# Four of eight modulation chunks: their products written for GpSimd instead of TensorE

## The chip, the cores and the metric

One core of one Trainium2 chip runs the kernel. Its engines run in parallel and each works through its own instructions in order: TensorE (PE in the profile, with its weight loads as PEld), VectorE (DVE), ScalarE (ACT), GpSimd (POOL), and SyncE (SP), whose queue issues the DMAs of this kernel. An instruction starts when everything it waits for, by semaphores, has happened; what stands behind it on its engine waits with it. The metric is the device time of one launch in microseconds (us), as the median of several runs. Times inside a run are from its profile and count from the start of the profiled span.

## The reference, cut to what matters

Two transformer blocks run one after the other on 512 tokens of width 1024. In the first one the vector `c` yields six modulation rows of 1024 numbers each. Two of them (`sh1`, `sc1`) shape the input of the attention; the other four are used after it:

```
m_lat = jax.nn.silu(c) @ w_mod[l] + b_mod[l]
sh1, sc1, g1, sh2, sc2, g2 = jnp.split(m_lat[:, None, :], 6, axis=-1)
...
y = merge_branches(proj, att, ...)      # gates, attention and convolution branches, output projection
x_mid = x + g1 * y
h2 = modulate(rmsnorm(x_mid, norm_ffn[l]), sh2, sc2)
f = hierarchical_moe(h2, ...)           # 32 experts, each a SwiGLU
x = x_mid + g2 * f
```

`w_mod` is 1024 x 6144 in float32. A row of the modulation is made in two chunks of 512 columns; a chunk needs 1024 x 512 weights (2 MB, in two loads of 1 MB), eight products of 128 x 512 with a number for each partition, and a sum over the 128 partitions, which at the same time spreads the row to all partitions.

## The kernel before

The kernel is written in program order; every engine gets its instructions in the order of the code, and a planner of the buffers gives each tile a place in one of 23 buffers of 8 KB a partition (pool `w`) or 6 of 4 KB (pool `h`). A DMA waits on SP until the earlier user of its buffer is done, and the DMAs behind it wait with it.

After the convolution's work, the last of 16 attention steps (`attention`, `s_work`) are interleaved with the gate projections `ga0` to `gb7` (`gate_proj`: eight k-steps of three matmuls each, and a tanh on ACT), and then the branch projections `ao0` to `ao7` follow (the loop over `i` with `pys`). Each of these takes a unit of the weight stream: SP loads it raw (`ga6r`), ACT rounds it to a high part and DVE makes the low part (`ga6p`, L200 and L270), and PE multiplies with both. `mr` is a tile with a chunk's sum in its first quarter and the bias row in its fourth; `bcs0` and `bcs1` hold the finished rows; `sil` holds silu of `c`.

The modulation's chunks go through these steps as a side job: `mod_run(n)` advances the generator `modr` by n steps, at most two in an attention step from number 13 on, four after each half of the gates 6 and 7, and one after each half of a branch. Eight chunks run one after the other, `g1`, `sc2`, `sh2`, `g2`, two each. A chunk of the first four has its eight products on DVE (L773, L775), is split into two parts there (`mt`, L202 and L207), and is summed over the partitions by two matmuls with ones (`mb`, L786 and L787). A chunk of the last four (`MOD_PE`) has its products on PE: eight matmuls in float32 (`mp`, L760, two instructions of each in the trace), a copy on ACT and a float32 matmul that sums (`mb`, L768). In both cases DVE then adds the bias row into `bcs` (L788). GpSimd computes nothing.

What comes behind is the output projection, the routing, the experts, whose 192 MB of weights are loaded as buffers come free, and the second block.

Of the kernel before, what the change touches and what calls it, by code (L numbers as in the profile page):

```python
# [9 lines left out]
F32R = mybir.dt.float32r  # L10
# [3 lines left out]
ALU = mybir.AluOpType  # L14
# [21 lines left out]

IN_H = [f"{nm}{n}" for nm in ("k_", "q_", "u_") for n in range(4)] + [f"m1{f}" for f in range(2, 32)]
N_HALF, N_LAST = 2, 4
MOD_PE = range(4, 8)
N_EARLY, N_PRE = 7, 15  # L40
N_KQ, N_V, N_C, N_A, N_M, N_MR, N_G, N_AO = 4, 1, 9, 7, 13, 2, 4, 1
WROW = 8
# [14 lines left out]
C_ID, C_TRI, C_ONE, C_SEL2, C_IOTA, C_RCNT, C_EOF, C_SELB, C_IOM8, C_IOM4, NC_ = 0, 128, 256, 384, 386, 514, 578, 706, 834, 842, 846  # L57
# [105 lines left out]
def body(ctx, tc, a, out, dbg=None):  # L163
# [8 lines left out]
    def slot(shape, name, dt=F32):  # L172

        return wpool.tile([P] + list(shape), dt, name=name, tag="w")

    def hslot(shape, name, dt=F32):

        return hpool.tile([P] + list(shape), dt, name=name, tag="h")

    def const(shape, name, dt=F32):  # L180
        return cpool.tile([P] + list(shape), dt, name=name)

    def bank(name, shape=(512,), parts=P):
        return pp.tile([parts] + list(shape), F32, name=name, tag="ps")
# [96 lines left out]
    cst = const([NC_], "cst")  # L281
# [26 lines left out]
    sil = const([KD, 32], "sil")  # L308
# [8 lines left out]
    ones_r = const([P], "ones_r", F32R)  # L317
# [425 lines left out]
    def mod_rows(n):
        nm, c = mod_todo[n]
        ch = mod_of[nm] + c
        if n == 0:
            mod_load(0, 0)
            mod_load(0, 1)
        cs = slice(512 * c, 512 * c + 512)
        t = slot([4, 512], f"mr{ch}")  # L750
        acc = t[:, 0]
        ld(t[:, 3], a["b_mod"][:, ch * 512:ch * 512 + 512].to_broadcast([P, 512]))
        if nm == "sc2" and c == 1:
            nf = slot([D], "nf")
            ld(nf, a["norm_ffn"].to_broadcast([P, D]))
        yield
        if n in MOD_PE:
            pm = bank(f"mp{ch}")
            for k in range(KD):
                mm(pm[32 * (k % 4):32 * (k % 4) + 32], sil[:, k, :], mod_w[n, k // 4][:, k % 4, :],  # L760
                   start=(k < 4), stop=(k >= 4), tile_position=(0, 32 * (k % 4)), skip_group_check=True)
                if k % 4 == 3:
                    del mod_w[n, k // 4]
                    mod_load(n + 1, k // 4)
# [4 lines left out]
        else:
            for k in range(KD):  # L770
                src = mod_w[n, k // 4][:, k % 4, :]
                if k == 0:
                    V.tensor_scalar(acc, src, sil[:, k, 0:1], None, op0=ALU.mult)  # L773
                else:
                    V.scalar_tensor_tensor(acc, src, sil[:, k, 0:1], acc, op0=ALU.mult, op1=ALU.add)  # L775
                if k % 4 == 3:
                    del mod_w[n, k // 4]
                    mod_load(n + 1, k // 4)
                if k % 2:
                    yield  # L780
            t2 = hslot([2, 512], f"mt{ch}", F32R)
            split(acc, t2[:, 0], t2[:, 1], V)
            yield
            yield
            ps = bank(f"mb{ch}")
            mm(ps, ones_r, t2[:, 0], start=True, stop=False)  # L786
            mm(ps, ones_r, t2[:, 1], start=False, stop=True)  # L787
        V.tensor_tensor(bc[nm][:, cs], ps, t[:, 3], op=ALU.add)  # L788
        if c == 1:
            if nm in ("g1", "g2"):  # L790
                V.tensor_scalar(bc[nm], bc[nm], 0.5, None, op0=ALU.mult)
            if nm == "sc2":
                V.scalar_tensor_tensor(bc[nm], bc[nm], 1.0, nf, op0=ALU.add, op1=ALU.mult)
        yield

    modr = chain(mod_rows(n) for n in range(len(mod_todo)))

    def mod_run(n):
        for _ in range(n):
            if next(modr, 0) == 0:  # L800
                return
# [47 lines left out]
    for i in range(8):  # L849
# [439 lines left out]
    for i, ps_ in enumerate(PASSES):  # L1289
# [28 lines left out]
        c = 0  # L1318
# [593 lines left out]
```

## Time and profile before

| what | us |
|---|---|
| median of 3 runs | 1513.46 (1513.39 to 1514.01) |
| the profiled execution | 1514.14 |
| its span, from the first to the last instruction | 1512.4 |
| PE busy | 1405.2 (93%) |
| DVE busy | 787.1 (52%) |
| ACT busy | 455.6 (30%) |
| POOL busy | 0.2, in 4 instructions |

The busy time of an engine is the time in which at least one of its instructions ran. Matmuls are pipelined: one of 128x512 stands with 0.39 us in the trace while the next one starts 0.23 us after it. The granted clock is the share of TensorE's full clock that it ran at. A wait is put down to what ended it last.

### The profile page before, as it was taken

To read this page: it belongs to the slowest core of one execution; us is meant where nothing else is said; L and a number is where in the kernel's file an instruction comes from. 1 tells how busy PE (TensorE), PEld (TensorE's weight loads), DVE (VectorE), ACT (ScalarE), POOL (GpSimd) and SP (SyncE) were. 2 spreads that over 40 slices of the span, in tenths; PEclk is the share of its full clock that TensorE was granted. 3 is DMA by queue.
4 is the path that set the end of the run, shared out by engine and by line. 5 is a ranking of instruction groups with operands and counts; after the bars stand their busy time and mean duration, and the time that the engine had idled before them with its cause. 6 is when DMAs were issued, how large, how long until landed. Compare 5 with 4: busy or idle time off the path is not lost. (4 is left out here: it accounts for less than half of the span.)

```text
span 1512.4 us, 18758 instructions
## 1 busy us (share of the span) xinstructions
PE 1405.2 (93%) x7398; PEld 973.0 (64%) x7398; DVE 787.1 (52%) x1559; ACT 455.6 (30%) x787; POOL 0.2 (0%) x4
## 2 busy tenths in 40 slices
PE   5999999999987989979999798899999999999997
PEld 4788877786773525334534254677678888878886
DVE  6387887586478423322333133746757443354326
ACT  4252566623231101101111012447723222343300
POOL 0000000000000000000000000000000000000000
PEclk9999999999997999989999899899999999999998
DMA  9232020688655899999999995131510222443301
GB/s 392 109 98 111 32 95 5 222 322 292 245 210 226 337 417 420 419 419 419 419 419 420 419 419 212 54 149 45 179 55 29 98 98 98 153 140 112 111 1 56
DMA packets 53243, 320.51 MB, mean 212 GB/s; under 512 B 6168, under 2 KB 6424, under 8 KB 21280
## 3 DMA queue, kind: packets, MB, share of 16 engines
q1 hardware_dynamic: 53152, 319.28, 54.0%
q8 instruction: 59, 0.97, 0.3%
q14 instruction: 32, 0.26, 0.0%
HBM read 317.15 MB, written 2.11 MB: 211 GB/s over the span
## 5 line engine op out<-in xcount | busy, mean ns | idle before, releaser
L1282 PE MATMUL pU<-wu,xT 128*64 128x512 f32 (+1 forms) x544 | 115.8, 638 | 22.1 <-DMA wu<-in_w_exp_up_dram 22.1
L1282 PE MATMUL py<-wd,mt 128*64 128x512 f32 (+1 forms) x544 | 107.6, 637 | 12.8 <-DMA wd<-in_w_exp_down_dram 7.6
L1282 PE MATMUL pG<-wg,xT 128*64 128x512 f32 (+1 forms) x544 | 95.5, 594 | 3.4 <-DMA wg<-in_w_exp_gate_dram 3.4
L1282 PEld LDWEIGHTS pU<-wu,xT 128*64 128x64 f32 (+1 forms) x544 | 32.5, 130 | 102.0 <-issue 57.9
L440 DVE SCALAR_TENSOR_TENSOR cacc<-u,cw,cacc 128x511 f32<-128x511 f32 (+14 forms) x120 | 89.1, 743 | 3.6
L1282 PEld LDWEIGHTS py<-wd,mt 128*64 128x64 f32 (+1 forms) x544 | 30.0, 131 | 81.5 <-issue 55.9
L1282 PEld LDWEIGHTS pG<-wg,xT 128*64 128x64 f32 (+1 forms) x544 | 29.7, 124 | 66.5 <-issue 56.9
L1734 DVE TENSOR_TENSOR hid<-rl 128x512 f32<-128x512 f32 x32 | 22.1, 692 | 96.2 <-ACT rl L1733 96.2
L1188 DVE TENSOR_TENSOR mt<-mt,pU 128x512 f32<-128x512 f32 x13 | 8.9, 688 | 110.9 <-PE pU L1282 110.8
L200 ACT ACTIVATE Cr<-pC 128x512 fp32r<-128x512 f32 x13 | 7.8, 598 | 187.0 <-PE pf L1204 179.4
L1205 DVE TENSOR_TENSOR xr<-xr,pf 128x512 f32<-128x512 f32 x96 | 58.4, 678 | 6.9 <-PE pf L1204 6.9
L1171 PE MATMUL px<-Db,yh 128*128 128x256 f32 x224 | 56.5, 292 | 2.6 <-DVE Db L1157 1.4
L576 ACT ACTIVATE at<-at,mx 128x512 f32<-128x512 f32 (+4 forms) x64 | 39.9, 624 | 62.5 <-DVE mx L665 28.4
L1733 ACT ACTIVATE rl<-m 128x512 f32<-128x512 f32 x32 | 19.1, 598 | 120.7 <-PE m L212 120.7
L1171 PE MATMUL px<-Db,yl 128*128 128x256 f32 x224 | 55.5, 287 | 0.0
L1197 DVE SCALAR_TENSOR_TENSOR mt<-py,gsl,bcs 128x512 f32<-128x512 f32 x26 | 19.5, 751 | 68.8 <-PE py L1282 68.7
L200 ACT ACTIVATE yb<-mt 128x512 fp32r<-128x512 f32 x26 | 16.4, 629 | 114.9 <-DVE mt L1197 114.9
L1187 DVE SCALAR_TENSOR_TENSOR mt<-mt,pG 128x512 f32<-128x512 f32 x13 | 8.9, 687 | 72.4 <-ACT mt L1186 72.4
L1171 PEld LDWEIGHTS px<-Db,yh 128*128 128x128 f32 x224 | 43.7, 195 | 4.3 <-ACT Cr L200 2.4
L1171 PEld LDWEIGHTS px<-Db,yl 128*128 128x128 f32 x224 | 43.8, 195 | 0.0
L1203 PE MATMUL pf<-yb,Cr 128*128 128x512 f32 x96 | 38.6, 402 | 0.0
L1204 PE MATMUL pf<-yb,Cr 128*128 128x512 f32 x96 | 37.6, 392 | 0.0
(1330 smaller groups left out, 3498.8 us busy)
## 6 DMA issues: line engine op xcount, KB each, us to landing
wg<-in_w_exp_gate_dram SPq DMA_DIRECT2D x64, 1024.0 KB, 19.8
wu<-in_w_exp_up_dram SPq DMA_DIRECT2D x64, 1024.0 KB, 19.8
wd<-in_w_exp_down_dram SPq DMA_DIRECT2D x64, 1024.0 KB, 19.8
wmod<-in_w_mod_dram SPq DMA_DIRECT2D x24, 1024.0 KB, 6.4
bias<-in_bias_dram SPq DMA_DIRECT2D x4, 896.0 KB, 5.3
x<-in_x_rows_dram SPq DMA_DIRECT2D x2, 1024.0 KB, 6.8
mr<-in_b_mod_dram SPq DMA_DIRECT2D x8, 256.0 KB, 5.9
xr<-in_x_rows_dram SPq DMA_DIRECT2D x2, 1024.0 KB, 7.2
```

The lines of the kernel that those rows point to most:

```text
L200: S.activation(dst, src, AF.Copy)
L440: V.scalar_tensor_tensor(cacc[:, i, lo_:hi_], u[:, i, lo_ + d:hi_ + d], w1, cacc[:, i, lo_:hi_], op0=ALU.mult, op1=ALU.add)
L576: S.activation(sb[:, 0:nk], sb[:, 0:nk], AF.Exp, bias=mx[:, s, 0:1], scale=score[2], accum_out=mx[:, s, 1:2])
L1171: mm(ps[:, k % 2], h_[t // 2][:, t % 2, k * P:(k + 1) * P], rhs, start=(k % 2 + t + n == 0), stop=(t == NT - 1 and n == 1), skip_group_che ...
L1187: V.scalar_tensor_tensor(t_, t_, 1.0, pG, op0=ALU.add, op1=ALU.mult)
L1197: V.scalar_tensor_tensor(yf, ps, gsl, bc["g2"][:, cs], op0=ALU.mult, op1=ALU.mult)
L1203: mm(ps, C[:, t * P:(t + 1) * P], y[0][:, cs], start=True, stop=False)
L1204: mm(ps, C[:, t * P:(t + 1) * P], y[1][:, cs], start=False, stop=True)
L1205: V.tensor_tensor(xrow[t][:, cs], xrow[t][:, cs], ps, op=ALU.add)
L1282: mm(ps[c:c + w], lhs[:, c:c + w], rhs(p), start=start, stop=stop, skip_group_check=True)
L1733: S.activation(r, ps, AF.Relu)
L1734: V.tensor_tensor(hid[f // 4][:, f % 4, :], r, r, op=ALU.mult)
```

## The change

The four chunks of `sh2` and `g2` are taken out of `modr`, which keeps `g1` and `sc2` (all on DVE), and go to a new generator, `pool_rows`. For each chunk it issues eight `tensor_scalar` and seven `tensor_tensor` on GpSimd (128x512, float32), each waiting for the one before it where it reads its result. DVE splits the finished chunk, PE sums it with two matmuls with ones, and DVE adds the bias, as the chunks of `modr` do. The first statement of `mod_run` advances `pool_rows` by one step in every call, so its chunks begin with the last attention steps; before, their matmuls were issued with the branches. The float32 matmuls `mp` and `mb` with `C_SELB` and the copies on ACT are gone.

```diff
-MOD_PE = range(4, 8)
-    mod_todo = [(nm, c) for nm in names for c in range(2)]
+    mod_todo = [(nm, c) for nm in ("g1", "sc2") for c in range(2)]
...
-        if n in MOD_PE:
-            pm = bank(f"mp{ch}")
-            for k in range(KD):
-                mm(pm[32 * (k % 4):32 * (k % 4) + 32], sil[:, k, :], mod_w[n, k // 4][:, k % 4, :],
...
-            copy(S, acc, pm)
-            yield
-            ps = bank(f"mb{ch}")
-            mm(ps, cst[:, C_SELB:C_SELB + P], acc, start=True, stop=True)
...
+    def pool_rows(todo):
+        old, w = None, {}
+        def load(n):
+            nm, c = todo[n]
+            w[n] = [load_mod(mod_of[nm] + c, half) for half in range(2)]
+        load(0)
+        yield
+        for n in range(len(todo) + 1):
+            if n < len(todo):
+                nm, c = todo[n]
+                ch = mod_of[nm] + c
+                t = slot([4, 512], f"mr{ch}")
+                ld(t[:, 3], a["b_mod"][:, ch * 512:ch * 512 + 512].to_broadcast([P, 512]))
+                for k in range(KD):
+                    src = w[n][k // 4][:, k % 4, :]
+                    G.tensor_scalar(t[:, min(k, 1)], src, sil[:, k, 0:1], None, op0=ALU.mult)
+                    if k:
+                        G.tensor_tensor(t[:, 0], t[:, 0], t[:, 1], op=ALU.add)
+                del w[n]
+                new = nm, c, ch, t
+            yield
+            if n + 1 < len(todo):
+                load(n + 1)
+            if old:
+                nm_, c_, ch_, t_ = old
+                t2 = hslot([2, 512], f"mt{ch_}", F32R)
+                split(t_[:, 0], t2[:, 0], t2[:, 1], V)
+                yield
+                ps = bank(f"mb{ch_}")
+                mm(ps, ones_r, t2[:, 0], start=True, stop=False)
+                mm(ps, ones_r, t2[:, 1], start=False, stop=True)
+                V.tensor_tensor(bc[nm_][:, 512 * c_:512 * c_ + 512], ps, t_[:, 3], op=ALU.add)
+                if nm_ == "g2" and c_:
+                    V.tensor_scalar(bc[nm_], bc[nm_], 0.5, None, op0=ALU.mult)
+            old = new
...
+    modp = pool_rows([(nm, c) for nm in ("sh2", "g2") for c in range(2)])
     def mod_run(n):
+        next(modp, 0)
...
     mod_run(100)
+    for _ in modp:
+        pass
```

In the tiles' names the number after `wmod`, `mr`, `mt` or `mb` is the chunk: 4 and 5 are `g1`, 8 and 9 `sc2`, 6 and 7 `sh2`, 10 and 11 `g2`; `_0` and `_1` are a chunk's two loads. SP's queue, at the first loads of the modulation, before:

```order
L295 DMA wmod4_0_2159<-in_w_mod_dram 128x2048 [waits DVE_49]
L295 DMA wmod4_1_2161<-in_w_mod_dram 128x2048 [waits DMAHW6_49,PE_49]
L752 DMA mr4_2163<-in_b_mod_dram 128x512 [waits DMAHW7_49,PE_49]
L254 DMA ga5r_2191<-in_stream1_dram 128x1024 [waits DMAHW0_49]
L295 DMA wmod5_0_2239<-in_w_mod_dram 128x2048 [waits DMAHW1_49,PE_49,Activation_49]
L254 DMA gb5r_2266<-in_stream1_dram 128x1024 [waits DMAHW2_49]
L295 DMA wmod5_1_2313<-in_w_mod_dram 128x2048 [waits DMAHW5_49,DMAHW3_49,DVE_49]
L254 DMA ga6r_2340<-in_stream1_dram 128x1024 [waits DMAHW4_49]
L254 DMA gb6r_2395<-in_stream1_dram 128x1024
```

The same queue now, from the bias row of the first GpSimd chunk on (the two loads of chunk 6 and those of chunk 4 stand ahead of it):

```order
L797 DMA mr6_2241<-in_b_mod_dram 128x512 [waits DMAHW3_49,PE_49]
L294 DMA wmod5_0_2260<-in_w_mod_dram 128x2048 [waits DMAHW7_49,DMAHW4_49,DVE_49]
L253 DMA gb5r_2287<-in_stream1_dram 128x1024 [waits DMAHW5_49]
L294 DMA wmod7_0_2332<-in_w_mod_dram 128x2048 [waits DMAHW6_49,DVE_49]
L294 DMA wmod7_1_2334<-in_w_mod_dram 128x2048 [waits PE_49,Activation_49]
L797 DMA mr7_2336<-in_b_mod_dram 128x512 [waits DMAHW0_49,Pool_49]
L294 DMA wmod5_1_2355<-in_w_mod_dram 128x2048 [waits DMAHW1_49,DVE_49]
L253 DMA ga6r_2382<-in_stream1_dram 128x1024 [waits DMAHW2_49]
L294 DMA wmod10_0_2411<-in_w_mod_dram 128x2048 [waits DMAHW6_49,DMAHW3_49,Pool_49]
L294 DMA wmod10_1_2413<-in_w_mod_dram 128x2048 [waits DMAHW4_49,PE_49,Activation_49]
L253 DMA gb6r_2444<-in_stream1_dram 128x1024 [waits DMAHW5_49]
```

Four loads of 1 MB and two bias rows now stand ahead of `ga6r` or between it and `gb6r`, and two of the DMAs wait for POOL. In the same way `wmod11_0`, `wmod8_0` (ahead of `gb7r`) and `wmod9_1` (ahead of `ao1r`) wait for POOL further on.

DVE, from the split of the first `g1` chunk to the first product of the second, before:

```order
L202 CAST mt4_2315<-mr4_2163 128x512 [waits DVE_49]
L207 TENSOR_TENSOR mt4_2315<-mr4_2163,mt4_2315 128x512 [waits DVE_49]
L270 TENSOR_TENSOR gb5p_2338<-gb5r_2266,gb5p_2338 128x1024 [waits DMAHW2_49,Activation_49]
L788 TENSOR_TENSOR bcs0_1048<-mb4_2369,mr4_2163 128x512 [waits DMAHW7_49,PE_49]
L270 TENSOR_TENSOR ga6p_2393<-ga6r_2340,ga6p_2393 128x1024 [waits DMAHW4_49,Activation_49]
L773 TENSOR_SCALAR mr5_2424<-wmod5_0_2239,sil_108 128x512 [waits DMAHW1_49]
```

The same place now:

```order
L201 CAST mt4_2357<-mr4_2167 128x512 [waits DVE_49]
L206 TENSOR_TENSOR mt4_2357<-mr4_2167,mt4_2357 128x512 [waits DVE_49]
L269 TENSOR_TENSOR gb5p_2380<-gb5r_2287,gb5p_2380 128x1024 [waits DMAHW5_49,Activation_49]
L201 CAST mt6_2415<-mr6_2241 128x512 [waits Pool_49]
L206 TENSOR_TENSOR mt6_2415<-mr6_2241,mt6_2415 128x512 [waits DVE_49]
L774 TENSOR_TENSOR bcs0_1048<-mb4_2418,mr4_2167 128x512 [waits DMAHW1_49,DMAHW7_49,PE_49,Pool_49]
L269 TENSOR_TENSOR ga6p_2442<-ga6r_2382,ga6p_2442 128x1024 [waits DMAHW2_49,Activation_49]
L816 TENSOR_TENSOR bcs1_1049<-mb6_2473,mr6_2241 128x512 [waits DMAHW3_49,DVE_49,PE_49]
L759 TENSOR_SCALAR mr5_2494<-wmod5_0_2260,sil_108 128x512 [waits DMAHW4_49,PE_49]
```

The split of chunk 6 and its bias stand between the weights' low parts, and two instructions ahead of `ga6p` wait for POOL. In the built program `bcs0` has the place in which `wmod7_1` lay, so the wait of L774 for POOL is for the last product of chunk 7 that reads it.

## Rows read from the trace of the kernel before

**Rows 1.** Page: busy us of each engine (share of the span), instructions.

```profile
PE 1405.2 (93%) x7398; PEld 973.0 (64%) x7398; DVE 787.1 (52%) x1559; ACT 455.6 (30%) x787; POOL 0.2 (0%) x4
```

**Rows 2.** Busy by stretch: stretch, us, engines, granted clock, DMA share, GB/s.

```profile
275.00:280.00 5.00, 3.17 (x16) 2.08 (x13) 4.05 (x10) 4.71 (x10) 0.00 (x0) 0.92 0.85 301
280.00:285.00 5.00, 5.00 (x18) 3.91 (x17) 4.19 (x10) 2.96 (x7) 0.00 (x0) 0.74 0.90 334
276.00:345.00 69.00, 66.38 (x322) 53.22 (x321) 50.52 (x73) 23.61 (x39) 0.00 (x0) 0.98 0.75 274
345.00:382.00 37.00, 36.20 (x183) 23.18 (x181) 24.64 (x34) 11.65 (x16) 0.00 (x0) 1.00 0.82 293
382.00:460.00 78.00, 72.43 (x410) 60.58 (x412) 44.05 (x160) 23.95 (x42) 0.00 (x0) 0.98 0.54 210
```

**Rows 3.** Groups of PE by line, 225 to 425 us: busy, mean ns, idle before.

```profile
L760 PE MATMUL mp<-wmod,sil 128*32 128x512 f32 x64 | 7.7, 598 | 0.0
L768 PE MATMUL mb<-mr,cst 128*128 128x512 f32 x8 | 4.2, 605 | 0.8 <-ACT mr L200 0.8
```

**Rows 4.** Groups of DVE by line, 276 to 345 us: busy, mean ns.

```profile
L775 DVE SCALAR_TENSOR_TENSOR mr<-wmod,sil,mr 128x512 f32<-128x512 f32 x27 | 20.3, 750 | 0.7
L207 DVE TENSOR_TENSOR mt<-mr,mt 128x512 fp32r<-128x512 f32 x4 | 2.8, 692 | 0.1
L202 DVE CAST mt<-mr 128x512 fp32r<-128x512 f32 x4 | 1.7, 426 | 0.1
L773 DVE TENSOR_SCALAR mr<-wmod,sil 128x512 f32<-128x512 f32 x3 | 1.4, 480 | 0.0
L270 DVE TENSOR_TENSOR ga6p<-ga6r,ga6p 128x1024 fp32r<-128x1024 f32 x1 | 1.2, 1225 | 1.8 <-ACT ga6p L200 1.8
L791 DVE TENSOR_SCALAR bcs<-bcs 128x1024 f32<-128x1024 f32 x1 | 0.7, 694 | 0.0
```

**Rows 5.** SP's queue in order of time: start, us, DMA.

```profile
262.71 0.80 SPq L295 DMA_DIRECT2D wmod<-in_w_mod_dram  x2
...
279.99 0.42 SPq L254 DMA_DIRECT2D ga6r<-in_stream_dram  x1
280.46 1.48 SPq L254 DMA_DIRECT2D gb6r<-in_stream_dram  x1
...
301.12 0.42 SPq L254 DMA_DIRECT2D gb7r<-in_stream_dram  x1
...
308.04 0.62 SPq L254 DMA_DIRECT2D ao1r<-in_stream_dram  x1
```

**Rows 6.** DMA issues: KB each, median us from issue to landing.

```profile
wmod<-in_w_mod_dram SPq DMA_DIRECT2D x24, 1024.0 KB, 6.4
v0r<-in_stream_dram SPq DMA_DIRECT2D x2, 512.0 KB, 3.4
```

**Rows 7.** PE in order of time: start, us, instruction.

```profile
275.09 0.60 PE L644 MATMUL as<-kvc,qT 64*128 64x256 f32 x4
...
292.52 0.39 PE L786 MATMUL mb<-mt,ones_r 128*128 128x512 f32 x1
292.76 0.39 PE L787 MATMUL mb<-mt,ones_r 128*128 128x512 f32 x1
...
301.81 0.50 PE L210 MATMUL ga<-hTh,ga6p 128*128 128x512 f32 x1
...
330.16 0.39 PE L210 MATMUL y<-at,ao1p 128*128 128x512 f32 x1
```

**Rows 8.** Who waited for whom, 270 to 345 us: total, times, longest.

```profile
PE gb L212 <- DVE gb4p L270: 1.8, 1, 1.8
PE y L212 <- DVE ao3p L270: 0.5, 1, 0.5
```

**Rows 9.** DVE in order of time, 276 to 345 us: start, us, instruction.

```profile
278.05 3.11 DVE L775 SCALAR_TENSOR_TENSOR mr<-wmod,sil,mr 128x512 f32<-128x512 f32 x4
...
295.69 1.23 DVE L270 TENSOR_TENSOR ga6p<-ga6r,ga6p 128x1024 fp32r<-128x1024 f32 x1 [1.81 <-ACT ga6p L200]
```

**Rows 10.** ACT in order of time: the high part of one weight unit.

```profile
294.60 1.06 ACT L200 ACTIVATE ga6p<-ga6r 128x1024 fp32r<-128x1024 f32 x1
```

More of the change, by code (lines that the diff above doesn't have):

```diff
@@ L756, in mod_rows @@
         yield
-        if n in MOD_PE:
-            pm = bank(f"mp{ch}")
-            for k in range(KD):
-                mm(pm[32 * (k % 4):32 * (k % 4) + 32], sil[:, k, :], mod_w[n, k // 4][:, k % 4, :],
[L761 to L764, printed above, removed]
-            copy(S, acc, pm)
-            yield
-            ps = bank(f"mb{ch}")
-            mm(ps, cst[:, C_SELB:C_SELB + P], acc, start=True, stop=True)
[L769 to L787, printed above, removed]
+        for k in range(KD):
+            src = mod_w[n, k // 4][:, k % 4, :]
+            if k == 0:
+                V.tensor_scalar(acc, src, sil[:, k, 0:1], None, op0=ALU.mult)
+            else:
+                V.scalar_tensor_tensor(acc, src, sil[:, k, 0:1], acc, op0=ALU.mult, op1=ALU.add)
+            if k % 4 == 3:
+                del mod_w[n, k // 4]
+                mod_load(n + 1, k // 4)
+            if k % 2:
+                yield
+        t2 = hslot([2, 512], f"mt{ch}", F32R)
+        split(acc, t2[:, 0], t2[:, 1], V)
+        yield
+        yield
+        ps = bank(f"mb{ch}")
+        mm(ps, ones_r, t2[:, 0], start=True, stop=False)
+        mm(ps, ones_r, t2[:, 1], start=False, stop=True)
         V.tensor_tensor(bc[nm][:, cs], ps, t[:, 3], op=ALU.add)
         if c == 1:
-            if nm in ("g1", "g2"):
+            if nm == "g1":
                 V.tensor_scalar(bc[nm], bc[nm], 0.5, None, op0=ALU.mult)
@@ L794, in mod_rows @@
         yield
+    def pool_rows(todo):
[4 more added lines that the diff above has]
+        load(0)
+        yield
+        for n in range(len(todo) + 1):
[4 more added lines that the diff above has]
+                ld(t[:, 3], a["b_mod"][:, ch * 512:ch * 512 + 512].to_broadcast([P, 512]))
+                for k in range(KD):
+                    src = w[n][k // 4][:, k % 4, :]
[4 more added lines that the diff above has]
+                new = nm, c, ch, t
+            yield
+            if n + 1 < len(todo):
[4 more added lines that the diff above has]
+                split(t_[:, 0], t2[:, 0], t2[:, 1], V)
+                yield
+                ps = bank(f"mb{ch_}")
+                mm(ps, ones_r, t2[:, 0], start=True, stop=False)
+                mm(ps, ones_r, t2[:, 1], start=False, stop=True)
+                V.tensor_tensor(bc[nm_][:, 512 * c_:512 * c_ + 512], ps, t_[:, 3], op=ALU.add)
+                if nm_ == "g2" and c_:
+                    V.tensor_scalar(bc[nm_], bc[nm_], 0.5, None, op0=ALU.mult)
+            old = new
     modr = chain(mod_rows(n) for n in range(len(mod_todo)))
+    modp = pool_rows([(nm, c) for nm in ("sh2", "g2") for c in range(2)])
     def mod_run(n):
+        next(modp, 0)
         for _ in range(n):
```

## The prediction

> **What bounds the kernel now.** I read the page first: PE is busy 93% of the span, POOL does nothing [rows 1]. Then the stretches. The chunks that the change takes lie at 345 to 382 us, where PE is busy 36.2 of 37.0 us, and the place to which their products go, 276 to 345 us, has PE at 66.4 of 69.0 us, DVE at 50.5 and the DMA engines at 0.75 of their time [rows 2]. So PE sets the pace in both, and the waits confirm it: two short ones of PE, 1.8 and 0.5 us, both for the low part of a weight unit that DVE had not finished [rows 8]. An us taken from PE here is an us won, and a weight unit that comes an us late is an us lost once its cover is used up. That cover is read from SP's queue against PE: `ga6r` is issued at 279.99 us [rows 5] and first used at 301.81 us [rows 7]; `ao1r` at 308.04 and 330.16 us. It is some 22 us for each unit, and the path from issue to use needs about 6 of them: landing 3.4 us for 512 KB [rows 6], 1.06 us on ACT [rows 10], 1.23 us on DVE [rows 9]. After this stage come output projection and routing; the experts' loads start when buffers come free, and at 382 to 460 us the DMA engines are at 0.54 [rows 2], so I expect a shift of the end of the branches to reach the end of the kernel whole.
>
> **What is removed.** The matmuls `mp` and the float32 `mb` cover 7.7 + 4.2 = 11.9 us of PE [rows 3], on the path. In their place come eight matmuls with ones, 0.23 us apart (292.52 and 292.76, [rows 7]), 1.8 us; they stand ahead of `ao1`, in a stretch that the next part finds waiting, and cost nothing there; without the waits they would cost their 1.8. ACT loses four copies, off the path. DVE gains four splits of 0.43 + 0.69 us [rows 4], 4.5 us; its eight additions of a bias row remain.
>
> **What a chunk costs on POOL.** Call it c: eight products with a number and seven additions, each behind the one before it. No row shows POOL at such work, so I bound it by DVE's rows of the same shape and of twice the size [rows 4]. At DVE's own pace it is 8 x 0.48 + 7 x 0.69 = 8.7 us. At the pace of the rows with twice the columns it is 8 x 0.69 + 7 x 1.23 = 14.1 us. If each of the 15 instructions also waits out one of DVE's of 0.75 us, it is 14.1 + 11.3 = 25.4 us. DVE works on 128x512 tiles from SBUF for much of this time: in the changed order some 18 products of `modr` (0.75 us), 8 low parts (1.23) and 7 subtractions (0.69) fall between the start of the first chunk and `ao1`, 13.5 + 9.8 + 4.8 = 28 us, 7 us for each chunk. I take c between no interference (14.1) and 14.1 + 7 = 21 us, which is 17.6, and 18 with a few hundredths for each hand-over; the ends 8.7 and 25.4 are kept for the range.
>
> The Trainium skill, GPSIMD Engine Reference, section 3.1, gives 4497 ns on GpSimd against 2293 on DVE for an addition of 2048 columns. Scaled to 512 columns that is an estimate of 1.1 us, near the 1.23 of the row with twice the columns; for a one-input product it gives no time.
>
> **What waits for POOL.** The first chunk starts when its place for the sum is free, after the scores of attention step 15, whose matmuls start at 275.09 us and run 0.60 [rows 7]: 276.0 us. Its loads, issued from 262.71 us on [rows 5], have landed by then (6.4 us) [rows 6]. The four chunks follow each other at 276 + c, 276 + 2c, 276 + 3c, and end at 276 + 4c. Behind them queue, by the order of the changed kernel:
> SP. `mr7` waits for the last product of chunk 6, and `wmod5_1` and `ga6r` stand behind it: issued at 276 + c instead of 280. `wmod10_0` waits for the middle of chunk 7, `gb6r` behind it. `wmod8_0` waits for the end of chunk 10, and `gb7r` behind it: 276 + 3c instead of 301.12 [rows 5]. `wmod9_1` waits for the last product of chunk 11, and `ao1r` behind it: 276 + 4c instead of 308.04.
> DVE. The split of chunk 6 waits for it; L774 waits for the last product of chunk 7, at 276 + 2c - 1.3, with the low part of `ga6` behind it: 276 + 2c + 0.6 for c = 18 is 312.6, and PE wants it at about 302.4, two matmuls after 301.81 [rows 7]. So PE loses 10 us there, and later stalls add only what exceeds it.
> The last of these settles the sum. After chunk 11 (276 + 4c): the load of 1 MB ahead of `ao1r` and `ao1r` itself land about 5 us later (between 3.4 and 6.4, [rows 6]), ACT 1.06, DVE 1.23 and 1.1 for the split of chunk 11, which stands behind `ao1`'s low part and ahead of which PE's sum of chunk 11 cannot run. That is 276 + 4c + 8.4. Before, PE began `ao1` at 330.16 us [rows 7]. With c = 18: 356.4, so 26.2 us later.
>
> **The sum**, against the profiled execution, 1514.1 us: + 26.2 (`ao1` late) - 11.9 (PE's products gone, all behind `ao1`) + 3 (DVE comes to `ao1` with more of the second `sc2` chunk undone: nine instructions, about 7 us, against 1.4 us of spare time in each of the next units) + 1 (after a stall of 1.8 us the granted clock was 0.92 and 0.74 in two stretches of 5 us [rows 2], 1.7 us lost; only what follows the last stall counts) = 1532.4. The median lies 0.7 below the profiled execution: **1532 us**. In general 1460 + 4c as long as POOL paces; it breaks even at c = 13.4. The other edits (order of the chunks, `bcs` written in another order) move nothing else.
>
> **Rivals.**
> *No interference, POOL at the pace of twice the columns.* c = 13.4 to 16: 1513 to 1524. For it: DVE itself would wait behind L774 for much of the time. Against it: POOL's chunks then run beside 28 us of DVE work on the same memory.
> *Exclusion or a slower POOL.* If POOL and DVE never read SBUF at the same time, c = 14.1 + 7 + 0.6 = 21.7 and the time is 1547; to c = 26 it is 1564. For it speaks that nearly all of DVE's work here reads two tiles from SBUF; no row can show it, since POOL is idle. The Trainium skill states just that: SBUF — State Buffer, section "Who interferes with whom", says a DVE instruction with two SBUF inputs and a GpSimd instruction that reads SBUF share a read interface, which one holds for a whole instruction while the other blocks. By that rule this rival is the one that happens.
> *POOL near DVE's pace: faster.* The mechanism is the cover of 22 us: with c below 13.4 the weights come in time. At c = 9 no weight unit is late by more than the shared places make it (`ga6p` now lies where `gb5p` and `ga5p` lay and `ga7p` where `gb6p` lay, so ACT and DVE prepare them only after the matmuls of the one before: about 0.7 and 1.4 us of PE, by 1.06 and 1.23 against the matmuls between). Then 1513.5 - 11.9 + 1.8 + 2.1 = 1505.5. It decides at c = 13.4, that is 1.5 times DVE's pace. Against it: 15 dependent instructions on an engine that must also hand over between each.
> *The delay is absorbed.* The experts' loads run at 0.54 of the DMA engines' time at 382 to 460 us [rows 2], and fill them later; if the loads, not the routing, set that stage's start, a late branch stage costs nothing: 1514. Against it: these loads go to buffers that the late units hold.
>
> **How the numbers follow.** The forecast (c 16 to 21, 1524 to 1545) has 0.42; exclusion or a slower POOL 0.25; no interference 0.17, of which 0.05 lies within 0.2% of the time before; POOL near DVE's pace 0.10; absorbed 0.06. The 0.2%, 3 us, is about what a measurement of this kernel tells from no change. So faster 0.10, same 0.11, slower 0.79. For 8 in 10 I leave out the faster case and the top of the slow one: 1514 to 1557 us.
>
> **What would show it.** In the profile after: POOL busy about 4c, 60 to 90 us, from 276 us on, without gaps; its additions longer than 0.69 us; SP's issues of `ga6r`, `gb7r` and `ao1r` behind ends of POOL's products, at about 294, 330 and 348 us; PE waiting for the low part of `ga6` with DVE behind POOL, for several us; DVE's instructions lengthened beside POOL's if the two exclude each other; the first `ao1` matmul near 356 us; no L760 group. I am wrong if POOL's chunks take under 13 us, if the units are not late though POOL is slow (the waits then end earlier than I read), or if the late branches leave the start of the experts where it was.

## The result and the profile after

The changed kernel takes 1563.36 us (1563.16 to 1565.32, 4 runs) against 1513.74 (1513.39 to 1514.13, 4 runs) of the kernel before: a ratio of 1.0326, 95% interval 1.0313 to 1.0339, slower. The forecast was 1532 us, in a range of 1514 to 1557: the sign is right, the size is not, and the time lies outside the range. The profiled execution took 1563.23 us, its span is 1561.4 us, 49.0 more than before.

The page first, the line of busy times that answers [rows 1]:

```profile
PE 1409.5 (90%) x7334; PEld 977.5 (63%) x7334; DVE 806.5 (52%) x1567; ACT 453.7 (29%) x783; POOL 96.9 (6%) x64
```

PE did not get less busy though 64 instructions are gone: it is stalled more often, and its granted clock is lower in the stretches with the stalls (0.80 and 0.73 below, 0.98 and 1.00 in [rows 2]). By stretches (us, then busy time of PE, PEld, DVE, ACT and POOL, granted clock, DMA share, GB/s; answers [rows 2]):

```profile
276.00:345.00 69.00, 45.16 (x209) 34.07 (x208) 37.56 (x46) 16.87 (x30) 64.67 (x41) 0.80 0.49 176
345.00:390.00 45.00, 25.16 (x78) 17.96 (x77) 23.39 (x27) 4.26 (x5) 32.07 (x20) 0.73 0.54 197
390.00:432.00 42.00, 39.38 (x170) 30.70 (x169) 33.73 (x45) 12.02 (x15) 0.00 (x0) 1.00 0.51 188
432.00:510.00 78.00, 70.84 (x397) 60.12 (x395) 43.55 (x155) 23.78 (x40) 0.00 (x0) 0.96 0.52 202
```

In the first 69 us PE is busy 45.2 where it was 66.4, while POOL is busy 64.7. DVE is less busy than before (37.6 against 50.5) and so are the DMA engines (0.49 against 0.75). But for POOL nothing is overloaded; things wait. From 390 us on the picture is that of before. Who waited, 276 to 390 us for SP and DVE, to 440 us for PE (total, times, longest; answers [rows 8]):

```profile
SPq L294 <- POOL mr L800: 64.8, 4, 22.5
SPq L797 <- POOL mr L800: 12.9, 1, 12.9
...
DVE bcs L774 <- POOL mr L800: 20.0, 1, 20.0
DVE mr L759 <- DMA wmod<-in_w_mod_dram: 11.2, 1, 11.2
...
PE ga L211 <- DVE ga6p L269: 14.4, 1, 14.4
PE gb L209 <- ACT gb7p L199: 14.1, 1, 14.1
PE ga L209 <- ACT ga6p L199: 3.7, 1, 3.7
PE mb L814 <- DVE mt L201: 3.4, 1, 3.4
```

PE itself never waits for POOL by name. It waits for weight units that DVE and ACT had not prepared. DVE stood in its own wait for POOL (20.0 us), and ACT had no weights because SP's queue stood 65 us in all behind loads (L294) into places that POOL was still reading. SP's issues, the same units as in [rows 5]:

```profile
302.53 0.42 SPq L253 DMA_DIRECT2D ga6r<-in_stream_dram  x1
...
352.00 0.42 SPq L253 DMA_DIRECT2D gb7r<-in_stream_dram  x1
...
354.24 23.31 SPq L294 DMA_DIRECT2D wmod<-in_w_mod_dram  x2
377.64 0.38 SPq L253 DMA_DIRECT2D ao1r<-in_stream_dram  x1
```

`ga6r` is 22.5 us late against [rows 5], `gb7r` 50.9, `ao1r` 69.6. PE's first matmul on `ao1`, the end of the chain that the prediction followed, answers the last line of [rows 7]:

```profile
387.54 0.63 PE L209 MATMUL y<-at,ao1p 128*128 128x512 f32 x1
```

It is 57.4 us late (387.54 against 330.16); the forecast had 26.2. POOL's work, by line and shape (busy us, mean ns), first all of it and then the second chunk alone, 303 to 325.7 us, in which DVE stood in its wait of 20.0 us:

```profile
L800 POOL TENSOR_SCALAR mr<-wmod,sil 128x512 f32<-128x512 f32 x32 | 59.1, 1850 | 279.1 <-DVE mx L661 276.7
L802 POOL TENSOR_TENSOR mr<-mr 128x512 f32<-128x512 f32 x28 | 37.7, 1347 | 2.3
...
L800 POOL TENSOR_SCALAR mr<-wmod,sil 128x512 f32<-128x512 f32 x8 | 12.8, 1598 | 0.6
L802 POOL TENSOR_TENSOR mr<-mr 128x512 f32<-128x512 f32 x8 | 10.1, 1267 | 0.7
```

(Of the eight additions in the second window one is the last of the chunk before, which ends as the window begins.) The chunks follow each other without a gap: by the trace they start at 277.17, 303.00, 325.75 and 352.44 us and the last ends at 378.61. That is 25.36 us each in the mean, 22.75 for the one that ran alone. The forecast had 18.

### The profile page after: what moved, and what is told of

It reads as the page before. It is cut to its first block, busy times and chain, and to the rows that moved or that the text cites. A ratio compares the mean times of both kernels' runs of the same rounds, so it can differ in the third digit from the quotient of the medians.

```text
span 1561.4 us, 18716 instructions
## 1 busy us (share of the span) xinstructions
PE 1409.5 (90%) x7334; PEld 977.5 (63%) x7334; DVE 806.5 (52%) x1567; ACT 453.7 (29%) x783; POOL 96.9 (6%) x64
## 5 line engine op out<-in xcount | busy, mean ns | idle before, releaser
L1311 PE MATMUL py<-wd,mt 128*64 128x512 f32 (+1 forms) x544 | 104.3, 632 | 11.8 <-DMA wd<-in_w_exp_down_dram 6.7
L1311 PE MATMUL pG<-wg,xT 128*64 128x512 f32 (+1 forms) x544 | 99.0, 616 | 3.7 <-DMA wg<-in_w_exp_gate_dram 3.7
L1311 PEld LDWEIGHTS py<-wd,mt 128*64 128x64 f32 (+1 forms) x544 | 29.4, 130 | 77.7 <-issue 56.4
L800 POOL TENSOR_SCALAR mr<-wmod,sil 128x512 f32<-128x512 f32 x32 | 59.1, 1850 | 279.1 <-DVE mx L661 276.7
L1232 PE MATMUL pf<-yb,Cr 128*128 128x512 f32 x96 | 38.6, 402 | 0.0
```

The source lines that it names most:

```text
L800: G.tensor_scalar(t[:, min(k, 1)], src, sil[:, k, 0:1], None, op0=ALU.mult)
L1232: mm(ps, C[:, t * P:(t + 1) * P], y[0][:, cs], start=True, stop=False)
L1311: mm(ps[c:c + w], lhs[:, c:c + w], rhs(p), start=start, stop=stop, skip_group_check=True)
```

## The experiments

Each kernel is an edit of the changed one, unless it says otherwise. "ao1" is the start of PE's first matmul on `ao1`; the last column is the span less that start. Span and starts are from the profiled execution, the times are medians over all executions, and the ratios go to the kernel before on the same chip.

| run | last chunk ends | ao1 | span | time | ratio (95%) | after ao1 |
|---|---|---|---|---|---|---|
| before | - | 330.16 | 1512.4 | 1513.7 | 1 | 1182.2 |
| after | 378.61 | 387.54 | 1561.4 | 1563.36 | 1.0326 (1.0313 to 1.0339) | 1173.9 |
| e5_quiet_dve | 375.35 | 384.27 | 1558.4 | 1559.16 | 1.0293 (1.0276 to 1.0310) | 1174.1 |
| e4_two_inputs | 365.49 | 374.70 | 1548.6 | 1550.55 | 1.0240 (1.0223 to 1.0257) | 1173.9 |
| e2_half_cols | 345.27 | 356.26 | 1529.7 | 1532.50 | 1.0120 (1.0104 to 1.0137) | 1173.4 |
| e1_eight_cols | 323.74 | 339.44 | 1514.2 | 1517.88 | 1.0028 (1.0019 to 1.0038) | 1174.8 |
| e12_small_loads | 322.49 | 341.24 | 1516.5 | 1517.21 | 1.0021 (1.0012 to 1.0031) | 1175.3 |
| e3_half_undone | 325.97 | 353.63 | 1532.2 | 1534.62 | 1.0132 (1.0115 to 1.0148) | 1178.6 |
| e6_apart | 390.95 | 345.49 | 1534.4 | 1535.59 | 1.0137 (1.0120 to 1.0154) | 1188.9 |
| e7_held | 400.66 | 346.29 | 1540.8 | 1539.93 | 1.0159 (1.0137 to 1.0181) | 1194.5 |
| e8_held_two | 398.13 | 352.36 | 1544.9 | 1546.52 | 1.0208 (1.0191 to 1.0225) | 1192.5 |
| e9_held_eight | 365.04 | 337.45 | 1518.6 | 1520.87 | 1.0050 (1.0033 to 1.0067) | 1181.2 |
| e10_half_held | 332.89 | 345.38 | 1528.9 | 1530.75 | 1.0121 (1.0104 to 1.0138) | 1183.5 |
| e11_beside | 380.60 | 338.51 | 1526.6 | 1527.40 | 1.0089 (1.0072 to 1.0106) | 1188.1 |

The first theory, A, is the prediction's own: what moves the end is that instructions of SP and DVE stand behind POOL's chunks.

**POOL's pace: shorter products.** Two kernels keep every instruction, wait and load and cut the width of what POOL computes.

```diff
-                    G.tensor_scalar(t[:, min(k, 1)], src, sil[:, k, 0:1], None, op0=ALU.mult)
+                    z = slice(0, 8 if k else 512)      # e2: 256 if k else 512
+                    G.tensor_scalar(t[:, min(k, 1), z], src[:, z], sil[:, k, 0:1], None, op0=ALU.mult)
                     if k:
-                        G.tensor_tensor(t[:, 0], t[:, 0], t[:, 1], op=ALU.add)
+                        G.tensor_tensor(t[:, 0, z], t[:, 0, z], t[:, 1, z], op=ALU.add)
```

> The changed kernel with seven of eight products and the additions of GpSimd on 256 of the 512 columns (half of those columns of sh2 and g2 left out). A TENSOR_SCALAR took 1.56 us and a TENSOR_TENSOR 1.27 us undisturbed; with half the columns about 0.8 and 0.65, so c = 1.6 + 7 x 1.45 + 15 x 0.09 = 13.1 us alone, 14 to 15 beside DVE. Theory A (time = 1460 + 4c): 1512 to 1520 us, about the kernel before. Theory B (the order of the queues, not POOL's speed): over 1535 us, near e1's time.

> The changed kernel with GpSimd's products cut short: of each chunk the first product covers all 512 columns, the other seven products and the seven additions only 8 columns (most of sh2 and g2 is left out). Every instruction, wait, load and place stays where it is in its queue; only the time of one chunk on POOL, c, falls from 25.4 us to 1.6 + 14 x (0.1 to 0.3) = 3 to 6 us. Theory A (the end moves because instructions of SP and DVE, queued behind POOL's chunks, wait for them; c is all that counts): POOL is no longer last, ao1 starts at 330 or a little earlier, the time is 1500 to 1512 us, and no wait of SP or DVE for POOL is over 3 us. Theory B (the new order of the queues costs the time whatever POOL's speed: loads issued later, places taken in another order): over 1535 us.

Both fell far, as A wants: POOL's speed is worth 45 of the 50 us. But both stopped short of the numbers. e2 took 1532.5 (1512 to 1520 expected): its half-width products still took 1.18 us in the mean and the chunks 17.1 us, so the price does not halve with the columns. By the prediction's own formula, 1460 + 4 x 17.1 is 1528; 4 us are missing. e1 took 1517.9 with POOL busy for 29 us in all: its chunks still come only every 12.1 us, since the second and the third wait for their weights (7.5 and 2.3 us) and the fourth for DVE (4.6), and SP still waits 11.3 us for the additions on POOL. So the expectation that a quick POOL makes the kernel faster (1500 to 1512) is wrong: ao1 is 9.3 us later than before (339.44 against 330.16), and POOL's computing alone does not explain it. On PE itself the 9.3 us read as 4.1 us more waiting ahead of ao1 (5.9 against 1.8, mostly for `gb5` and `gb7`), 1.8 us for four more sums that now stand there, and an estimated 1.7 us at a granted clock of 0.66 from 325 to 330 us, behind the wait for `gb7`; the rest is open.

**POOL's pace: the form of the product.** The product with one input is the dearer instruction (1598 against 1267 ns undisturbed). e4 writes it with two.

```diff
-                    G.tensor_scalar(t[:, min(k, 1)], src, sil[:, k, 0:1], None, op0=ALU.mult)
+                    G.tensor_tensor(t[:, min(k, 1)], src, sil[:, k, 0:1].to_broadcast([P, 512]), op=ALU.mult)
```

> The changed kernel with the one-input product on GpSimd (tensor_scalar with a column of sil) written as a product of two tensors (tensor_tensor, the column of sil read with step 0). Undisturbed 15 x 1.27 + 15 x 0.09 = 20.4 us a chunk, beside DVE 22 to 24 (the changed kernel: 25.4 in the mean). Theory A: 1460 + 4 x 23 = 1552 us (1546 to 1557). If the price of the product is not in its form but in what it reads (a weight tile just landed), its mean stays at 1.8 us and the time at 1563.

1550.55 us, 12.8 faster than the changed kernel, as A had it. POOL's groups:

```profile
L802 POOL TENSOR_TENSOR mr<-mr 128x512 f32<-128x512 f32 x28 | 42.5, 1519 | 2.2
L800 POOL TENSOR_TENSOR mr<-wmod,sil 128x512 f32<-128x512 f32 x32 | 41.5, 1302 | 278.9 <-PE as L643 277.0
...
304.70 1.04 POOL L800 TENSOR_TENSOR mr<-wmod,sil 128x512 f32<-128x512 f32 x1
```

The product went from 1850 to 1302 ns, the addition from 1347 to 1519; a chunk is 22.0 us. The last row is one of the products of the second chunk, from 304 to 318 us, where DVE stood in a wait and nothing disturbed POOL: 1.04 us where the one-input form had 1.56 in the same place. The same work in the other form is 13% cheaper on POOL, and the end follows POOL.

**POOL's pace: DVE's products.** e5 cuts DVE's own products of `g1` and `sc2` to 8 columns.

```diff
+                z = slice(0, 8)
-                V.scalar_tensor_tensor(acc, src, sil[:, k, 0:1], acc, op0=ALU.mult, op1=ALU.add)
+                V.scalar_tensor_tensor(acc[:, z], src[:, z], sil[:, k, 0:1], acc[:, z], op0=ALU.mult, op1=ALU.add)
```

> The changed kernel with VectorE's own products of the other four chunks (g1, sc2) cut to 8 columns, except the first of each chunk (most of g1 and sc2 left out): 28 instructions of 0.75 to 1.1 us go from VectorE, no queue changes. Theory A with a slowdown of POOL while VectorE works beside it: c falls from 25.4 to what it was in the one undisturbed chunk, 22.8 us, and the time to 1460 + 4 x 22.8 = 1551 us (1546 to 1556); DVE's other work beside POOL may keep c at 23.5. If POOL's pace does not depend on these products: c stays 25 and the time 1560 to 1564. If VectorE's load itself is what sets the end: below 1540.

1559.16 us, 4 less than the changed kernel; 8 more than the middle of the expectation. A chunk took 24.5 us, not 22.8. So DVE's products account for about 0.8 of the 2.6 us by which POOL's chunks exceed the undisturbed one; the rest was not taken apart. It is a small term. DVE's 8-column products show how the two engines meet (min/median/max in ns):

```profile
L762 DVE SCALAR_TENSOR_TENSOR mr<-wmod,sil,mr x21: 211/234/1297, 279.6 to 371.2; 128x8 f32<-128x8 f32 x21
...
L762 DVE SCALAR_TENSOR_TENSOR mr<-wmod,sil,mr x6: 218/224/228, 383.5 to 391.3; 128x8 f32<-128x8 f32 x6
```

The first row is beside POOL, the second after POOL's end. Most are not delayed at all, and a few wait a whole microsecond, which is within the length of one instruction of POOL.

**Half of the change undone.** In e3 only `sh2`'s two chunks are on POOL, `g2`'s on PE as before.

```diff
-    mod_todo = [(nm, c) for nm in ("g1", "sc2") for c in range(2)]
+    mod_todo = [(nm, c) for nm in ("g1", "sc2", "g2") for c in range(2)]
...
-    modp = pool_rows([(nm, c) for nm in ("sh2", "g2") for c in range(2)])
+    modp = pool_rows([(nm, c) for nm in ("sh2",) for c in range(2)])
```

> Half of the change undone: only the two chunks of sh2 are multiplied on GpSimd (begun at 277 us as in the changed kernel), those of g2 on TensorE again, as before. Theory A (the delay is that of the instructions queued behind POOL): in SP's queue the load of the bias row of chunk 5, and behind it the gate weights ga7, wait for the end of the second chunk, some 277 + 49 = 326 us, so ga7 starts near 333, ao1 two gates and one branch later, 352 to 358; behind ao1 TensorE has g2's products again, so about 1179 us follow: 1531 to 1538 us, half of the loss. Rival (what costs is the first chunk's start, whose load and places meet the gate weights, and later chunks add little): over 1548. Rival (most is lost in the last chunks): below 1522.

1534.62 us with ao1 at 353.63: both in the expected windows. SP's longest wait and what stands behind it are the mechanism, read directly:

```profile
SPq L751 <- POOL mr L813: 21.8, 1, 21.8
...
324.36 0.33 SPq L751 DMA_DIRECT2D mr<-in_b_mod_dram  x1
324.79 0.38 SPq L253 DMA_DIRECT2D ga7r<-in_stream_dram  x1
```

The bias row waits for chunk 7's products, and `ga7r`, which has nothing to do with POOL, is issued 0.4 us after it, 38 us later than the 286 us of the kernel before.

**The waits taken away.** If A were all, the same work on POOL with nothing queued behind it should cost nothing. e6 writes each step that needs a chunk's result or place later, by a list of steps; e7 also keeps the places from being handed on, by two one-column copies on DVE from the weight tiles in the step that splits the chunk.

```diff
+    PLAN = {0: 'load0', 1: 'mul0', 5: 'load1', 6: 'mul1', 8: 'free0 half0', 9: 'row0 load2', 10: 'mul2',
+            13: 'free1 half1', 14: 'row1', 16: 'load3', 17: 'mul3', 20: 'free2 half2', 21: 'row2', 25: 'free3 half3 row3'}
...
+        def free(n):
+            for i in range(2):                                                        # e7 alone
+                V.tensor_copy(rows[n][:, 2, i:i + 1], w[n][i][:, 0, 0:1])             # e7 alone
+            del w[n]
```

> The changed kernel with the same work on GpSimd, but each step that needs a chunk's result or place written later: the chunk's split on VectorE 7 calls after its products (it was 3), loads of the next chunk's weights 4 calls after the products were issued and no longer right behind them, the last split behind the last branch. The planner still gives wmod6's places to ga5p and to bcs, so ga5's split waits for the middle of chunk 0 (about 289 us, it ran at 286) and the first row of g1 for its end (302 us, it ran at 293). Theory A (waits behind POOL are all): SP no longer waits for POOL over 5 us, only these two places cost, some 3 to 10 us at ao1: ao1 at 332 to 342, the time 1510 to 1520 us. Rival B (POOL's work beside VectorE slows it so much that the end moves whatever the queue): over 1530 us.

> e6 with the places held too: in the step that splits a chunk VectorE copies one column of each weight tile (two instructions of about 0.1 us a chunk), so the planner gives these places to nobody before that step. GpSimd's work is the same, 4 chunks of 25 us from 277 to about 380 us. Theory A: no instruction of SP, ACT or VectorE waits for POOL over 1 us before 375 us; ao1 at 328 to 333 us; behind it TensorE lacks the 7.5 us of products; the last chunk ends at about 380 where the branches end at 376 to 382, so up to 4 us may be lost there: 1505 to 1513 us, as fast as the kernel before or a little faster. Rival B (slowed VectorE, clock, places): over 1525 us.

The time falls by 28 and 23 us, but not to the kernel before: 1535.6 and 1539.9. In e6 the waits for POOL are fewer but not gone: SP still has one of 7.7 us, and ACT two, one of which PE then feels:

```profile
ACT ao0p L199 <- POOL mr L799: 13.5, 1, 13.5
ACT ga5p L199 <- POOL mr L799: 6.7, 1, 6.7
...
PE y L209 <- ACT ao0p L199: 6.2, 1, 6.2
```

So e6 does not put theory A to the test; e7 does, and A does not cover its 1539.9. In e7 no wait for POOL over 1 us is left on SP, ACT or DVE; what stands in their place (PE's largest wait, then DVE's busy time by stretches of 15 us, columns as above):

```profile
PE mb L817 <- DVE mt L201: 9.6, 2, 5.9
...
330.00:345.00 15.00, 12.05 (x45) 9.21 (x45) 14.69 (x16) 2.71 (x3) 14.27 (x9) 0.89 0.82 306
345.00:360.00 15.00, 10.60 (x40) 8.01 (x39) 13.76 (x15) 1.57 (x2) 14.47 (x9) 0.85 0.54 220
360.00:375.00 15.00, 11.14 (x37) 8.42 (x36) 12.82 (x17) 1.58 (x2) 14.27 (x10) 0.81 0.62 227
```

DVE is busy 41.3 of 45 us and PE 33.8, and PE's largest wait is for DVE: DVE sets the pace. The span behind ao1 is 20 us longer than in the changed kernel. This asked for a second theory, C: DVE's instructions, stretched beside POOL, are the next bound.

**A quicker POOL with the waits gone.** e8 is e7 with e4's form of the product.

> e7 with the one-input product on GpSimd written with two inputs (22 instead of 25 us a chunk). Theory A: POOL ends at about 366, before the last branch, nothing waits for it: 1503 to 1511 us, at most 3 us below e7, since POOL's pace counts only where something waits for it. If POOL's pace counts by itself (by VectorE's slowdown or TensorE's clock), e8 lies some 10 us below e7, as the same edit did in the changed kernel (13 us).

Neither came: e8 is 6.6 us slower than e7 (1546.5 against 1539.9), where the same edit had won 12.8 in the changed kernel. DVE's products, 320 to 400 us, in e7 and then in e8:

```profile
L761 DVE SCALAR_TENSOR_TENSOR mr<-wmod,sil,mr 128x512 f32<-128x512 f32 x14 | 14.8, 1059 | 0.4
...
L761 DVE SCALAR_TENSOR_TENSOR mr<-wmod,sil,mr 128x512 f32<-128x512 f32 x14 | 20.3, 1450 | 0.4
```

0.75 us alone, 1.06 beside POOL's one-input products, 1.45 beside its two-input ones. POOL's cheaper form is the one that stretches DVE most. Where POOL paces, it is worth having; where DVE paces, it costs. This speaks for C.

**POOL's work by itself.** e11 is the kernel before with POOL doing as much work beside it that nobody waits for.

```diff
+    d = bc["g2"].rearrange("p (a b) -> p a b", a=2)
+    def beside(bias):
+        for k in range(30):
+            G.tensor_scalar(d[:, min(k, 1)], bias if k < 2 else d[:, 1], sil[:, k % KD, 0:1], None, op0=ALU.mult)
+            if k:
+                G.tensor_tensor(d[:, 0], d[:, 0], d[:, 1], op=ALU.add)
...
                 if k % 2:
+                    if n == 0 and k == 1:
+                        beside(t[:, 3])
                     yield
```

> The kernel before, with the work that the change gives to GpSimd put beside it as idle work: 30 one-input products and 29 additions of 128x512 on the row that g2's result fills later, from about 270 us on, on which nothing waits before 370 us (the products of sh2 and g2 stay on TensorE). It shows what GpSimd's work costs VectorE by itself. Theory A (only waits behind POOL count): within 4 us of the kernel before, 1511 to 1518 us. Theory C (VectorE, slowed beside POOL, becomes the bound by itself): its products at 1.0 to 1.2 us (0.75 before), 27 of them and their neighbours 10 to 20 us more in 276 to 382 us, where it had 26 us free: 1518 to 1535 us.

1527.40 us, 13.9 more than the 1513.52 of before beside it: C, in the middle of its window. This is the disputed cost alone: POOL's presence, with nothing held up by a wait for it, is 14 us. (One wait of ACT, 4.2 us, is put down to POOL; it had the same one for PE before, 4.1 us.) Stretches of 10 us, first before, then in e11, then two groups of DVE, 276 to 382 us, and PE's largest waits, all in e11:

```profile
310.00:320.00 10.00, 10.00 (x46) 8.23 (x45) 7.98 (x11) 2.57 (x4) 0.00 (x0) 1.00 0.64 258
320.00:330.00 10.00, 10.00 (x46) 8.23 (x45) 9.03 (x13) 2.07 (x3) 0.00 (x0) 1.00 0.99 382
330.00:340.00 10.00, 10.00 (x46) 8.29 (x45) 8.84 (x14) 1.58 (x2) 0.00 (x0) 1.00 0.90 313
...
310.00:320.00 10.00, 9.27 (x39) 6.77 (x38) 9.76 (x12) 2.33 (x3) 9.55 (x6) 1.00 0.77 301
320.00:330.00 10.00, 7.64 (x35) 6.04 (x33) 9.75 (x10) 3.09 (x4) 9.54 (x6) 1.00 0.68 248
330.00:340.00 10.00, 9.47 (x33) 7.02 (x34) 9.86 (x10) 0.00 (x0) 9.55 (x6) 0.83 0.61 237
...
L782 DVE SCALAR_TENSOR_TENSOR mr<-wmod,sil,mr 128x512 f32<-128x512 f32 x27 | 32.3, 1196 | 0.7
L872 DVE SCALAR_TENSOR_TENSOR sg<-sg,y 128x512 f32<-128x512 f32 x10 | 6.4, 675 | 1.4 <-PE y L212 1.4
...
PE y L210 <- ACT ao3p L200: 2.9, 1, 2.9
PE mb L795 <- DVE mt L202: 2.7, 2, 2.4
```

Before, DVE was busy 8.0, 9.0 and 8.8 us in these three stretches and PE 10.0 in each. With POOL beside it DVE is full, and PE drops to 7.6. The 27 products took 32.3 us where [rows 4] has 20.3. One more thing differs in e11: the tile that POOL writes (`bcs0`) is in use some 20 us earlier, and `ga6r` is issued 6.5 us later (286.51 against 279.99). No wait of PE is for that unit, so the trace shows nothing of the 14 us there.

**The places by themselves.** e9 is e7 with POOL's products on 8 columns (as in e1).

> e7 (steps apart, places held; 1540 us where theory A wanted at most 1513) with GpSimd's products on 8 columns, except the first of each chunk (most of sh2 and g2 left out). It parts the two causes that e7 leaves. Theory C (VectorE, slowed beside POOL, is the bound in e7: it was busy 41 of 45 us from 330 to 375): with POOL nearly idle VectorE is back at 0.75 us a product, 1505 to 1516 us. Theory D (the places held longer and the loads written elsewhere delay the gate weights: gb7r issued at 316 us, 301 in the kernel before): 1525 us or more.

1520.87 us, between the two windows, and DVE's products are back at 0.75 us (276 to 382 us):

```profile
L761 DVE SCALAR_TENSOR_TENSOR mr<-wmod,sil,mr 128x512 f32<-128x512 f32 x27 | 20.3, 752 | 0.7
```

e7 is 1.59% over the kernel before, e9 0.50%: some 24 and 7.5 us. So two thirds of e7's loss go with POOL's computing (C), and 7.5 us, what PE saves already taken off, stay with places and loads (D). If the two add, e11's 13.9 us and e9's 7.5 make up e7's 24 but for some 3 us.

**Half of the change, waits gone.**

> Half of the change, in e7's manner: the two chunks of sh2 on GpSimd with steps apart and places held, those of g2 on TensorE as before. TensorE saves 3.8 us; GpSimd works 50 us, from 277 to about 327. Theory A: 1508 to 1514 us. Theory C or D (VectorE slowed, or places held): half of e7's loss, 1520 to 1530 us.

1530.75 us, just above the window of C or D (1520 to 1530): half of the work on POOL costs not half of e7's loss but some 17 of its 24 us, and what makes it more was not taken apart. It is no better than e3 by more than 4 us: even two chunks, without a wait on POOL, cost 17 us where they save 3.8 us of PE. No version of the idea tried here comes below the kernel before.

**What is left when POOL is quick.** e12 is e1 with the loads of POOL's weights cut to a quarter.

```diff
-            w[n] = [load_mod(mod_of[nm] + c, half) for half in range(2)]
+            w[n] = [slot([4, 512], f"wmod{mod_of[nm] + c}_{half}") for half in range(2)]
+            for half in range(2):
+                ld(w[n][half][:, 0:1], a["w_mod"][mod_of[nm] + c, half][:, 0:1])
```

> e1 (GpSimd's products on 8 columns, 1517.9 us, ao1 at 339.4 us where the kernel before had 330.2) with the eight weight loads of GpSimd's chunks cut from 1 MB to 256 KB each (one of four rows of 512 columns of each tile is read, the rest of the weights is left out); queue order, instructions and places stay, but for two places that swap. It asks what is left of the loss when POOL is quick. Theory E (4 x 2 MB of weights, moved from 345 us on to 276 to 322 us, delay the gate weights behind them in the queue): ao1 at 328 to 333 us, 1506 to 1511 us, faster than the kernel before by the products that TensorE is rid of. Theory F (the places, and the order of the queue): ao1 at 336 to 340 us, 1514 to 1519 us.

1517.21 us, ao1 at 341.24: the time is in the window of theory F, ao1 1.2 us behind it. With a quarter of these loads' bytes ao1 comes no earlier than in e1 (339.44), so theory E, the traffic, is out. SP still waits for POOL, here in the order of the longest totals, 276 to 345 us:

```profile
SPq L790 <- POOL mr L803: 8.9, 2, 5.9
...
SPq L790 <- POOL mr L805: 8.1, 1, 8.1
```

The loads of each chunk wait for a place that the chunk before gives free, and the gate weights wait behind them in the same queue, so a chunk still comes only every 11.5 us with POOL busy for 8 of them. Which of the places is the decisive one, and how much of the delay is the POOL time that is left, was not taken apart further.

## Why the prediction was right or wrong

**The price of a chunk, c = 18: wrong, and it is the whole miss.** The step is "What a chunk costs on POOL". Measured 25.36 us, at the very end of its bounds (25.4). Term by term, from the undisturbed chunk: 8 products took 1.598 us where the forecast put 0.69, + 7.3 us; 7 additions 1.267 for 1.23, + 0.3; 14 hand-overs of 0.08 us for "a few hundredths", + 1.1. That is 22.75 for 14.1. The interference was over-, not undersized: + 2.6 us a chunk where the forecast added 3.5 (half of the 7 us of DVE work). The error was to give POOL's one-input product DVE's price for one with twice the columns. On DVE the one-input form is the cheaper one, 0.48 against 0.69 [rows 4]; on POOL it is the dearer one, and 3.3 times DVE's time. The two-input form, for which the row with twice the columns stood in, was right within 3%. A row for one form says nothing about another form on another engine.

**The formula 1460 + 4c: right where POOL paces.** With the measured c it gives 1561.4; the time is 1563.4. From the trace: start 277.17 (276.0 forecast), four chunks 101.44, from the last chunk's end to ao1 8.93 (8.4 forecast). Of the 57.4 us at ao1 the forecast had 26.2; 4 x 7.36 = 29.4 of the missing 31.2 are c, 1.2 the start, 0.5 the tail. Behind ao1 8.3 us come back (1182.2 to 1173.9), 7.9 by the forecast (11.9 - 3 - 1); only this sum was measured, its three terms were not, so they may be right by luck. That figure is the same to 1.4 us in after, e1, e2, e4 and e5.

**What waits for POOL: right.** Each of the named waits is in the trace: `ga6r` behind the first chunk, `gb7r` behind the third, `ao1r` behind the fourth, L774 with `ga6`'s low part behind it (20.0 us on DVE, 14.4 on PE). e3 and e7 confirm it from both sides.

**The rivals.** "Exclusion or a slower POOL" (1547 to 1564, chance 0.25) is what happened, by its second half: a slower POOL. For the exclusion itself, see below. "The delay is absorbed" fell: the 49.0 us reach the end whole. "POOL near DVE's pace: faster" (1505.5, chance 0.10) did not come even with POOL's computing cut to 29 us: e1 is 0.28% slower than before, and e9 0.5%. The break-even at c = 13.4 was therefore wrong as well: the formula's floor is not the kernel before less PE's products, because, as e1 and e12 read, the loads of the four chunks wait for each other's places and hold the gate weights behind them.

**The term that was hidden: DVE's slowdown.** The forecast gave it 3 us, as a backlog. In the changed kernel it costs nothing that can be seen, since DVE waits for POOL anyway (37.6 us busy of 69). Taken by itself it is 14 us (e11), more than the 11.9 us that PE is rid of. Of what is left once nothing waits for POOL it is the larger part (places and loads: 7.5 us, e9), and in the changed kernel the waits covered it.

**The range.** It ended at 1557, below the upper bound of c that the text itself had worked out, 25.4 (1561.6 by the formula). Leaving out "the top of the slow case" left out the answer.

## What to carry to other kernels

Work moved to GpSimd has three prices, to be asked in this order: how long it takes there in exactly the form that is issued (here 22.8 us a chunk for work that cost PE 3), what stands behind it in every in-order queue, by results and by the places that its operands hold (SP's loads here), and what it takes from VectorE beside it. Take the waits away only after looking at what is next: here VectorE, busy 33.8 of 40 us from 310 to 350 us before, had no room for instructions stretched by half. And where the bounds of an unmeasured price are wide, the range has to go to their ends.

## What the runs showed of the hardware that was not expected

- GpSimd's product of a 128x512 tile with a number per partition takes 1.56 to 1.6 us undisturbed, its sum of two tiles 1.27; VectorE has it the other way round (0.48 and 0.69). Written as a product of two tensors, one of them read with step 0, the mean fell from 1850 to 1302 ns in place (e4), undisturbed from 1.56 to 1.04 us.
- Who is slowed on VectorE depends on where it reads. Products on two tiles in SBUF went from 0.75 us to 1.06 (e7) and 1.45 (e8), and the CAST of the split, with one input, from 0.43 [rows 4] to 1.08 (e7, 330 to 375 us). The gate's product `sg<-sg,y`, which reads one tile from PSUM, kept its time: 675 ns in e7, e8 and e11, 680 before. Not each instruction that can be slowed is: `sg<-sg`, with two tiles in SBUF, took 0.69 us before, 1.06 in e7 (330 to 375 us) and 0.71 in e11 (276 to 382 us). The Trainium skill, SBUF — State Buffer, section "Who interferes with whom", says that a DVE instruction with two SBUF inputs contends with GpSimd and one with at most one SBUF input, outside its faster modes, does not, and that casts can enter such a mode; as to who can be slowed these rows agree.
- The two do not exclude each other wholly. In e7, from 330 to 375 us, POOL ran 14 products and 12 additions (the first and the last reach over the edges), some 36 us at their undisturbed 1.56 and 1.26; DVE's instructions without a PSUM input came to some 24 us at their times of before. That is some 60 us of work in 45 us. The same section says that the one that comes second blocks for the other's whole instruction; by that rule the two sums would not fit into the stretch, and the measurement decides. Three of the groups of this stretch, the first of which is the CAST above:

```profile
L201 DVE CAST mt<-mr 128x512 fp32r<-128x512 f32 x4 | 4.3, 1084 | 0.1
...
L799 POOL TENSOR_SCALAR mr<-wmod,sil 128x512 f32<-128x512 f32 x14 | 26.6, 1904 | 1.1
L801 POOL TENSOR_TENSOR mr<-mr 128x512 f32<-128x512 f32 x12 | 18.2, 1518 | 1.0
```

- The prediction's page on prices, GPSIMD Engine Reference in the Trainium skill, section 3.1, gave an estimate of 1.1 us for the addition; the trace has 1.27.
